# Attention scores of the first query block: two key tiles side by side in one matmul

## The chip, the cores and the metric

The kernel runs on one core of one Trainium2 chip. Its time is device microseconds (us) of one execution; the kernel before takes 1036.5 us (median of 3 runs, 1036.27 to 1037.15). Engines are named as the profile names them: PE (matmul), PEld (weight load), DVE (vector), ACT (scalar), POOL and SP (SP issues most DMAs). Each engine works through its own instructions in the order in which the program holds them.

## The reference

One decoder layer on x of 512 rows by 1024 columns, float32: a half-step gated feed-forward block, a mixer, a second half-step feed-forward block, and a final norm. The mixer has one projection whose columns are split into attention query, key and value, a small indexer, a recurrent branch and gates:

```python
def one_block(args):
    q_b, qi_b, wi_b, start = args
    ...
    _, idx = lax.top_k(score, topk)
    valid = idx <= q_pos[None, :, None]
    k_sel = jax.vmap(lambda kk, ii: kk[ii])(k, idx)
    ...
    sc = jnp.einsum("bqhd,bqkd->bqhk", q_b, k_sel).astype(jnp.float32) * (HEAD_DIM ** -0.5)
    sc = jnp.where(valid[:, :, None, :], sc, -jnp.inf)
    p = jax.nn.softmax(sc, axis=-1)
    return jnp.einsum("bqhk,bqkd->bqhd", p.astype(v.dtype), v_sel)
```

There are 8 heads of 64, all on one key and value, four blocks of 128 queries, and 128 keys are kept for each query. For the first block that is every causal key.

## The kernel before, in words

Matmul operands are held as two tiles of a rounded type: the rounded part (names ending in h or H) and what the rounding left (l or L). A product of two such numbers is three matmuls. Weights come in as `wr`, ACT rounds them to `wh`, DVE makes the remainder `wl`; so each weight tile of 128 x 1024 costs ACT and DVE one long instruction, and PE 24 matmuls of 512 columns.

The mixer is a list of jobs (ORDER in the code). Each job multiplies one weight tile by the eight input tiles and leaves a bank of results: letters i, k, e, v, x, q, g, r, a are columns of the input projection, R0 to R7 the projection of the recurrent branch, A0 to A7 that of the attention, O0 to O7 the output. All work that is not such a product (indexer, top-k, attention heads, recurrent branch) is written as generators. Between any three of a job's matmuls the program asks each generator whether its next step is due. This is decided while the program is built, by a planner: it adds up a cost for every instruction on each engine and lets a step be written down when its inputs, a psum bank, a buffer and a slot would be there, and when its engine is not booked too far ahead. So every step's place in each engine's order follows from the costs of all that stand before it. If a job needs a tile that no generator has yet written, the builder lets planned time pass without a product (`idle`) and writes down what comes due meanwhile.

A head (`head`, four at most at a time) goes through these steps for one block of queries: PE makes the score of queries against keys, two matmuls into one bank, `KH` and then `KL`, at least 256 columns wide; DVE adds the mask `am` and takes the row minimum (`pm`, custom instruction; queries are stored negated); ACT takes the exponential and its sum; DVE the reciprocal; ACT scales `pm`; PE transposes it (one per 128 keys); ACT rounds the transposed tile to `pth`, DVE makes the remainder `ptl`. When four heads are there, PE multiplies `pth` and `ptl` with the values (`VV`); ACT copies the upper half (`lo`) and DVE adds the halves into the four attention tiles. A block of queries can only begin when `top_keys` has found its kept keys on DVE: 16 rounds of MAX and MATCH_REPLACE for each block but the first. The blocks are worked one after the other. When the last head has ended, `split_attention` rounds the four attention tiles (`ath`, `atl`), and job A0 uses them.

`KH` and `KL` are made in `key_value`: each is a tile of 128 x 512 that holds the 64 key dimensions twice, so that one matmul against `QS` (rounded query in one half of the partitions, remainder in the other) sums both.

Of the kernel before, what the change touches and what calls it, by code (L numbers as in the profile page):

```python
# [10 lines left out]
F32R = mybir.dt.float32r  # L11
AF = mybir.ActivationFunctionType
# [8 lines left out]
NH = 8  # L21
HD = 64
TOPK = 128
QB = 128
# [232 lines left out]
def hybrid_kernel(ctx, tc, xt, vec, w1s, w1u, w1d, wm, wki, wrg, watt, wrnn, wout, w2u, w2d, gf, out):  # L257
    nc = tc.nc
    plan = Plan()
    V, A = plan.engine("DVE", nc.vector), plan.engine("ACT", nc.scalar)  # L260
    G, T = plan.engine("POOL", nc.gpsimd), plan.engine("PE", nc.tensor)
# [16 lines left out]
    f = lambda ap: ap.bitcast(F32)  # L278
# [5 lines left out]
    def nm(s):  # L284
        cnt[0] += 1
        return f"{s}_{cnt[0]}"

    def slot(dt=F32, name="s", last=False):
        if loans and last:
            return loans.pop()  # L290
        if mixing:
            plan.free("slot", SLOTS - 2 * COUPLES)
            held = plan.live["slot"]
            spare = [h for h in mixing if plan.key(h) not in held]
            if spare and dt is F32:
                return plan.take("slot", spare[-last])
        return plan.take("whole", plan.take("slot", big.tile([P, S], dt, tag="slot", name=nm(name))))
# [4 lines left out]
    def work(name="t", cols=S):  # L302
        return plan.take("tmp", tmp.tile([P, cols], F32, tag="tmp", name=nm(name)))

    def awork(name="a"):
        return patt.tile([P, S], F32, tag="att", name=nm(name))
# [74 lines left out]
    def waits(which, *tiles, aux=0, att=0, slots=0, key=None, mm=0, tmps=0, late=LATE, rounded=0):  # L381
        return which, tiles, aux, att, slots, key, mm, tmps, late, rounded
# [979 lines left out]
    with tc.manual_schedule(engines=ENGINES):  # L1362
# [12 lines left out]
        for k in range(KD):  # L1375
            r, h, l = (t[:, slice(k % 2 * FIRST, min(2, k % 2 + 1 + (k > 1)) * FIRST)] for t in firsts[k // 2])
# [270 lines left out]
    def aux():  # L1647
        return plan.take("aux", psaux())
# [4 lines left out]
    def att(name):  # L1653
        return plan.take("att", awork(name))
# [94 lines left out]
    def head(qb, half, j, out, before):  # L1749
        am = AM[qb]  # L1750
        nk = (qb + 1) * QB
        nw = max(nk, 2 * QB)
        qs = slice(qb * QB, (qb + 1) * QB)
        h = half * 4 + j
        KH, KL = KV
        vvv = VV[0].rearrange("p (b c) -> p b c", c=P)
        yield waits("PE", QS[h], KL, aux=1)
        sc = aux()
        T.matmul(sc[:, :nw], QS[h][:, qs], KH[:, :nw], start=True, stop=False)
        T.matmul(sc[:, :nw], QS[h][:, qs], KL[:, :nw], start=False, stop=True)  # L1760
        yield waits("DVE", sc, am, att=1)
        pm = att("pm")
        st = small.tile([P, 4], F32, tag="st", name=nm("st"))
        V.tensor_tensor_reduce(pm[:, :nk], sc[:, :nk], am[:, :nk], HD ** -0.5, 3.4e38,
                               ALU.add, ALU.min, st[:, 0:1])
        plan.drop(sc)
        if h == NH - 1:
            plan.drop(am)
        if qb == NQ - 1:
            plan.drop(QS[h])  # L1770
            if h == NH - 1:
                plan.drop(KH, KL)
        yield waits("ACT", pm)
        A.activation(pm[:, :nk], pm[:, :nk], AF.Exp, scale=-1.0, bias=st[:, 0:1], accum_out=st[:, 1:2])
        yield waits("DVE", pm)
        V.reciprocal(st[:, 2:3], st[:, 1:2])
        yield waits("ACT", st)
        A.activation(pm[:, :nk], pm[:, :nk], AF.Copy, scale=st[:, 2:3])
        yield waits("PE", pm, aux=1)
        pt = aux()  # L1780
        for b in range(qb + 1):
            T.transpose(pt[:, b * QB:(b + 1) * QB], pm[:, b * QB:(b + 1) * QB], ident)
        plan.drop(pm)
        yield waits("ACT", pt, key=before)
        if not out:
            out["n"] = 0
            for k in ("pth", "ptl"):
                out[k] = ptp.tile([P, NQ * S], F32R, tag=k, name=nm(k)).rearrange("p (b c) -> p b c", c=S)
        pth, ptl = out["pth"], out["ptl"]
        c = slice(j * QB, (j + 1) * QB)  # L1790
        p3 = pt[:, :nk].rearrange("p (b c) -> p b c", c=QB)
        A.activation(pth[:, :qb + 1, c], p3, AF.Copy)
        yield waits("DVE", pth)
        V.tensor_sub(ptl[:, :qb + 1, c], p3, f(pth[:, :qb + 1, c]))
        plan.drop(pt)
        out["n"] += 1
        if out["n"] < 4:
            return
        yield waits("PE", ptl, aux=1)
        po = aux()  # L1800
        for b in range(qb + 1):
            T.matmul(po, vvv[:, b, :], pth[:, b, :], start=b == 0, stop=False)
            T.matmul(po, vvv[:, b, :], ptl[:, b, :], start=False, stop=b == qb)
        if qb == NQ - 1 and half:
            plan.drop(VV[0])
        yield waits("ACT", po, att=1)
        ready.add((qb, half))
        lo = att("lo")
        A.activation(lo[0:64, :], po[64:128, :], AF.Copy)
        yield waits("DVE", lo)  # L1810
        v4 = lambda ap: ap[0:64, :].rearrange("p (r s c) -> p r s c", r=2, s=2)
        for r in range(2):
            for s in range(2):
                V.tensor_add(ATT[half * 2 + r][s * 64:(s + 1) * 64, qs], v4(po)[:, r, s, :], v4(lo)[:, r, s, :])
        plan.drop(po, lo)
# [5 lines left out]
    def tick():  # L1821
        for item in list(follow):
            while due(item) and advance(follow, item):
                pass
        moved = True
        while moved:
            moved = False
            heads = sum(i[2] for i in active)
            if todo and ready >= {"QS", "index"} and todo[0][0] in AM and heads < HEADS:
                qb, half, j = todo.pop(0)  # L1830
                n = qb * 2 + half - 1
                before = None if n < 0 else (n // 2, n % 2)
                active.append([None, head(qb, half, j, outs.setdefault((qb, half), {}), before), 1, SLACK])
            for item in sorted(active, key=lambda i: -i[2]):
                if due(item, item[3]):
                    moved = advance(active, item) or moved
# [111 lines left out]
    for k in ("pth", "ptl"):  # L1948
        q = ptp.tile([P, NQ * S], F32R, tag=k, name=nm("QI"))
        QI.extend(q[:, j * S:(j + 1) * S] for j in range(4))  # L1950
    KV, VV, QS = [], [], []
    gates, ATT, rnn, hrec, RN, SGR, SGA, M, MS, y2 = [], [], [], [], [], [], [], [], [], []
    YN = []

# [69 lines left out]
    def key_value(ps):  # L2024
        yield waits("DVE", ps, rstd, key="KI", tmps=1)
        kv, kw = work("kv"), joint.pop()
        V.tensor_mul(kw[64:128, :], ps[64:128, :], rstd[64:128, :])
        V.tensor_mul(kv[0:64, :], ps[0:64, :], rstd[0:64, :])
        plan.drop(ps)
        yield waits("PE", kw, aux=1, slots=3, rounded=3)  # L2030
        KH, KL = slot(F32R, "KH"), slot(F32R, "KL")
        KV.extend((KH, KL))
        VV.append(slot(F32R, "VV"))
        pv = aux()
        for b in range(NQ):
            T.transpose(pv[:, b * QB:(b + 1) * QB], kw[:, b * QB:(b + 1) * QB], ident)
        plan.drop(kw)
        for o in (slice(0, 64), slice(64, 128)):
            A.activation(KH[o, :], kv[0:64, :], AF.Copy)
        yield waits("ACT", pv)  # L2040
        vvv = VV[0].rearrange("p (b c) -> p b c", c=P)
        blocks = pv.rearrange("p (b c) -> p b c", c=QB)
        pvv = blocks[:, :, 64:128]
        A.activation(vvv[:, :, 0:64], pvv, AF.Copy)
        for o in (slice(0, 64), slice(64, 128)):
            V.tensor_sub(KL[o, :], kv[0:64, :], f(KH[0:64, :]))
        plan.drop(kv)
        V.tensor_scalar(wi.rearrange("p (b c) -> p b c", c=8), blocks[:, :, 32:40], 8 ** -0.5, 32 ** -0.5,
                        op0=ALU.mult, op1=ALU.mult)
        ready.add("wi")  # L2050
        yield waits("DVE", VV[0])
        V.tensor_sub(vvv[:, :, 64:128], pvv, f(vvv[:, :, 0:64]))
        plan.drop(pv)
# [232 lines left out]
    def split_attention():  # L2286
# [15 lines left out]
        "i": lambda t: (y, index_query(t)),  # L2302
        "k": lambda t: (y, index_key),
        "v": lambda t: (y, key_value),
        "e": lambda t: (y, merge_gate(SGR, True)),
        "q": lambda t: (yn, query(t)),
# [265 lines left out]
```

## Time and profile before

| what | value |
|---|---|
| time, median of 3 runs | 1036.5 us |
| span of the profiled execution, first to last instruction | 1034.5 us |
| PE busy in the span | 1027.6 us, 5600 matmuls |
| DVE / ACT busy in the span | 906.6 / 710.4 us |
| first and last score matmul (KH) | 454.9 and 622.7 us (start of weight load) |
| first matmul on the attention tiles (`ath`) | 639.06 us |

Of the profiled execution the span is what is known; it is 2.0 us shorter than the median of the runs. A timeline row gives start, duration, engine, line (L251 is the recording helper that all operations go through), operation, the tile written and the tiles read, sizes, and how many instructions are merged; in square brackets stands the idle time of that engine before it and what ended it. Matmuls are pipelined: their rows overlap, and what one costs PE is the distance from its start to the next start. A row of a group gives the count, the busy time in all, the mean duration in ns and the idle time before.

### The profile page before, as it was taken

What the parts mean: (1) busy time and instruction counts of PE and PEld (TensorE: products, weight loads), DVE (VectorE), ACT (ScalarE), POOL (GpSimd) and SP (SyncE); (2) the same over time, 40 slices, a digit from 0 to 9 for tenths busy, and PEclk for the clock granted to TensorE, in tenths of its full rate; (3) what the DMA queues carried; (4) which work ended last, traced back from release to release, by engine and by line L of the source; (5) the groups of instructions that cost most, each with busy time, mean ns of one, the idle gap of its engine ahead of it and who ended that gap; (6) DMA issues with size and microseconds to landing.
All of it is one profiled execution on the core that took longest, in us unless ns stands there. A gap on an engine that the chain in (4) does not pass through costs nothing.

```text
span 1034.5 us, 16004 instructions
## 1 busy us (share of the span) xinstructions
PE 1027.6 (99%) x5600; PEld 892.9 (86%) x5600; DVE 906.6 (88%) x1571; ACT 710.4 (69%) x1195; POOL 203.3 (20%) x255
## 2 busy tenths in 40 slices
PE   9999999999999999999999999999999999999997
PEld 8898888899999888888888888888988888898886
DVE  7988999889998888998989966777889999989886
ACT  8856766666766669978896674367666766657864
POOL 1613333213240011111101110013432333110000
PEclk9999999999999999999999999999999999999999
DMA  9969999897994463343469987793889999987564
GB/s 355 201 171 216 222 238 216 192 275 194 183 244 152 149 181 101 107 128 107 122 187 282 278 212 209 208 295 62 193 226 245 215 221 227 205 203 225 167 189 164
DMA packets 92257, 206.01 MB, mean 199 GB/s; under 512 B 18576, under 2 KB 25872, under 8 KB 92176
## 3 DMA queue, kind: packets, MB, share of 16 engines
q1 hardware_dynamic: 59952, 141.75, 41.0%
q0 software_dynamic: 31936, 62.93, 35.0%
q8 instruction: 44, 0.72, 0.3%
q10 hardware_dynamic: 288, 0.31, 0.1%
q14 instruction: 37, 0.30, 0.1%
HBM read 185.02 MB, written 25.17 MB: 203 GB/s over the span
## 4 chain that ended last, share of the span: by engine, by line
PE 99%; DVE 0%; DVEq 0%; issue 0%
PE mm L251 72%; PE aux L251 27%; PE aux L1340 0%; DVE xr L251 0%; DVE o L251 0%; DVE sq L251 0%; DVEq L2568 0%; DVE rs L251 0%; DVE ss L251 0%
## 5 line engine op out<-in xcount | busy, mean ns | idle before, releaser
L251 DVE TENSOR_TENSOR wl<-wr,wh 128x1024 fp32r<-128x1024 f32 (+3 forms) x154 | 183.0, 1189 | 30.6 <-ACT wh L251 30.1
L251 ACT ACTIVATE wh<-wr 128x1024 fp32r<-128x1024 f32 (+2 forms) x155 | 158.8, 1026 | 43.4 <-PE mm L251 20.0
L251 PE MATMUL mm<-cm,wh 128*128 128x512 f32 (+1 forms) x736 | 167.0, 354 | 0.0
L251 PEld LDWEIGHTS mm<-cm,wh 128*128 128x128 f32 x736 | 126.3, 190 | 15.8
L251 PE MATMUL mm<-yn,wh 128*128 128x512 f32 x420 | 130.8, 393 | 0.0
L251 PE MATMUL aux<-cm,wh 128*128 128x512 f32 (+1 forms) x472 | 119.5, 383 | 0.0
L251 PE MATMUL mm<-cm,wl 128*128 128x256 f32 x608 | 108.3, 282 | 0.0
L251 PEld LDWEIGHTS aux<-cm,wh 128*128 128x128 f32 x472 | 86.0, 188 | 15.6
L251 PEld LDWEIGHTS mm<-cm,wl 128*128 128x128 f32 x608 | 92.2, 190 | 4.7
L251 PEld LDWEIGHTS mm<-yn,wh 128*128 128x128 f32 x420 | 77.0, 188 | 14.8
L251 PE MATMUL mm<-yn,wl 128*128 128x512 f32 x210 | 81.9, 390 | 0.0
L251 PE MATMUL aux<-cm,wl 128*128 128x256 f32 x456 | 70.5, 282 | 0.0
L251 ACT ACTIVATE wh<-a 128x1024 fp32r<-128x1024 f32 (+1 forms) x68 | 57.1, 842 | 18.2 <-DVE a L251 17.2
L251 DVE TENSOR_TENSOR wl<-a,wh 128x1024 fp32r<-128x1024 f32 (+1 forms) x68 | 64.7, 952 | 5.5 <-ACT wh L251 5.0
L251 PE MATMUL mm<-yh,wh 128*128 128x512 f32 (+1 forms) x168 | 65.4, 392 | 0.0
L251 PE MATMUL mm<-yl,wh 128*128 128x512 f32 (+1 forms) x168 | 65.3, 390 | 0.0
L251 PEld LDWEIGHTS aux<-cm,wl 128*128 128x128 f32 x456 | 63.1, 191 | 1.9
L251 PE MATMUL mm<-yh,wl 128*128 128x512 f32 x160 | 62.1, 390 | 0.0
L251 ACT ACTIVATE tu<-mm 128x512 f32<-128x512 f32 (+1 forms) x57 | 28.2, 495 | 43.8 <-PE mm L251 43.7
L251 DVE TENSOR_TENSOR wl<-s,wh 128x1024 fp32r<-128x1024 f32 (+1 forms) x46 | 49.3, 1080 | 1.2 <-ACT wh L251 1.1
L251 ACT ACTIVATE wh<-s 128x1024 fp32r<-128x1024 f32 (+1 forms) x46 | 43.0, 943 | 7.1 <-PE mm L251 2.0
L251 PEld LDWEIGHTS mm<-yn,wl 128*128 128x128 f32 x210 | 39.4, 188 | 8.5
(400 smaller groups left out, 2596.8 us busy)
## 6 DMA issues: line engine op xcount, KB each, us to landing
wr<-wm SPq DMA_DIRECT2D x39, 512.0 KB, 3.6
w<-w2d SPq DMA_DIRECT2D x20, 512.0 KB, 7.0
wr<-w SPq DMA_DIRECT2D x20, 512.0 KB, 3.5
wr<-w1u SPq DMA_DIRECT2D x19, 512.0 KB, 5.9
s<-w2u SPq DMA_DIRECT2D x36, 256.0 KB, 4.4
wr<-w2u SPq DMA_DIRECT2D x18, 512.0 KB, 5.6
s<-w2u POOLq DMA_DIRECT2D x36, 256.0 KB, 6.3
s<-w1u SPq DMA_DIRECT2D x32, 256.0 KB, 4.8
```

What stands on the lines that cost most here:

```text
L251: return call(*args, **kw)
```

## The change

For the first query block only 128 keys can be seen, and yet the two score matmuls run 256 columns each. The change makes one more tile `KB`: its first 128 columns are a copy of the first 128 of `KH` (by ACT), the next 128 a copy of the first 128 of `KL` (by DVE). A head of the first block then runs one matmul of 256 columns against `KB`, which leaves the two parts of the score in two halves of the bank; a new DVE addition puts the second half and the mask into `pm`, and the custom instruction adds the first half to that. The other three blocks are as before. `key_value` asks for four free slots where it asked for three.

```diff
-        yield waits("PE", QS[h], KL, aux=1)
+        yield waits("PE", QS[h], KB[0], KL, aux=1)
         sc = aux()
-        T.matmul(sc[:, :nw], QS[h][:, qs], KH[:, :nw], start=True, stop=False)
-        T.matmul(sc[:, :nw], QS[h][:, qs], KL[:, :nw], start=False, stop=True)
+        if qb:
+            T.matmul(sc[:, :nw], QS[h][:, qs], KH[:, :nw], start=True, stop=False)
+            T.matmul(sc[:, :nw], QS[h][:, qs], KL[:, :nw], start=False, stop=True)
+        else:
+            T.matmul(sc[:, :nw], QS[h][:, qs], KB[0][:, :nw], start=True, stop=True)
+            if h == NH - 1:
+                plan.drop(KB[0])
         yield waits("DVE", sc, am, att=1)
-        pm = att("pm")
+        pm, added = att("pm"), am
+        if not qb:
+            V.tensor_add(pm[:, :nk], sc[:, nk:nw], am[:, :nk])
+            added = pm
         st = small.tile([P, 4], F32, tag="st", name=nm("st"))
-        V.tensor_tensor_reduce(pm[:, :nk], sc[:, :nk], am[:, :nk], HD ** -0.5, 3.4e38,
+        V.tensor_tensor_reduce(pm[:, :nk], sc[:, :nk], added[:, :nk], HD ** -0.5, 3.4e38,
                                ALU.add, ALU.min, st[:, 0:1])
...
-        yield waits("PE", kw, aux=1, slots=3, rounded=3)
+        yield waits("PE", kw, aux=1, slots=4, rounded=4)
         KH, KL = slot(F32R, "KH"), slot(F32R, "KL")
         KV.extend((KH, KL))
+        KB.append(slot(F32R, "KB"))
...
+        A.activation(KB[0][:, :QB], f(KH[:, :QB]), AF.Copy)
...
+        V.tensor_copy(KB[0][:, QB:2 * QB], f(KL[:, :QB]))
```

All places after the first score move with it, since the planner books the new instructions. Three places in the order matter here.

The first is PE at the first four heads of the first block, in the middle of a job on `yn`. Before:

```order
L251 MATMUL mm_5184<-yn_4144,wl_5107 128x512
L251 MATMUL aux_5199<-KH_4362,QS_4488 128x256
L251 MATMUL aux_5199<-KL_4363,QS_4488 128x256
L251 MATMUL aux_5202<-KH_4362,QS_4489 128x256
L251 MATMUL aux_5202<-KL_4363,QS_4489 128x256
L251 MATMUL aux_5205<-KH_4362,QS_4559 128x256
L251 MATMUL aux_5205<-KL_4363,QS_4559 128x256
L251 MATMUL aux_5208<-KH_4362,QS_4560 128x256
L251 MATMUL aux_5208<-KL_4363,QS_4560 128x256
L251 MATMUL mm_5184<-yn_4169,wh_5106 128x512 x2
```

Now:

```order
L251 MATMUL mm_5187<-yn_4144,wl_5110 128x512
L251 MATMUL aux_5202<-KB_4364,QS_4491 128x256
L251 MATMUL aux_5204<-KB_4364,QS_4492 128x256
L251 MATMUL aux_5206<-KB_4364,QS_4562 128x256
L251 MATMUL aux_5208<-KB_4364,QS_4563 128x256
L251 MATMUL mm_5187<-yn_4169,wh_5109 128x512 x2
```

The first heads stand at the same place, with half the matmuls. From here on the heads come later: the fifth, sixth and seventh head of the first block stood 49, 52 and 67 product matmuls behind the first four and now all stand 73 behind; the first score of the fourth block stood 559 behind and now stands 634 behind. On DVE the last of the 48 MAX rounds stood behind the 83rd `wl` of the program and now stands behind the 86th.

The second place is PE at the end of the attention. Before, the last score pair stood 57 product matmuls ahead of the first matmul on `ath`, and the last product with `VV` 21 ahead. Right ahead of `ath` stood products of job R7:

```order
L251 MATMUL mm_6960<-rh_6428,wl_6843 128x512
L251 MATMUL mm_6960<-rh_6442,wh_6842 128x512
L251 MATMUL mm_6960<-rl_6443,wh_6842 128x512
L251 MATMUL mm_6960<-rh_6442,wl_6843 128x512
L251 MATMUL mm_6960<-rh_6454,wh_6842 128x512
L251 MATMUL mm_6960<-rl_6455,wh_6842 128x512
L251 MATMUL mm_6960<-rh_6454,wl_6843 128x512
L251 MATMUL mm_7025<-ath_6989,wh_6925 128x512
```

Now the last three matmuls of R7 (`mm_6842<-rh_6376` and the two after it) are followed by attention alone. `pm_6880` is the fourth head of the last query block, `pm_6904` the fifth:

```order
L251 MATMUL mm_6842<-rh_6376,wh_6696 128x512
L251 MATMUL mm_6842<-rl_6377,wh_6696 128x512
L251 MATMUL mm_6842<-rh_6376,wl_6697 128x512
L251 MATMUL aux_6932<-ident,pm_6880 128x128 x4
L251 MATMUL aux_6945<-ident,pm_6904 128x128 x4
L251 MATMUL aux_6951<-pth_6856,VV_4365 128x512
L251 MATMUL aux_6951<-ptl_6857,VV_4365 128x512
```

Six more products of the same kind follow, and then the sixth head's transposes, the score pair of the eighth head, the transposes of the seventh and eighth, and the second half's products:

```order
L251 MATMUL aux_6951<-ptl_6857,VV_4365 128x512
L251 MATMUL aux_6960<-ident,pm_6913 128x128 x4
L251 MATMUL aux_6979<-KH_4362,QS_5184 128x512
L251 MATMUL aux_6979<-KL_4363,QS_5184 128x512
L251 MATMUL aux_6985<-ident,pm_6942 128x128 x4
L251 MATMUL aux_6995<-ident,pm_6982 128x128 x4
L251 MATMUL aux_7002<-pth_6968,VV_4365 128x512
```

Behind seven more of these stands the first matmul on `ath`. So between the last product of R7 and A0 there are now 20 transposes, 2 score matmuls and 16 products with `VV`, and no product of a job among them.

The third place is DVE in the same stretch, from the fourth head's remainder to the eighth head's reduction; `hb_104` and `hb_106` are attention tiles in their additions and the latter is the mask in the ISA rows (the custom instruction):

```order
L251 TENSOR_TENSOR ptl_6857<-aux_6932,pth_6856 128x4x128
L251 ISA pm_6942,st_6943<-aux_6922,hb_106 128x512
L251 ISA st_6943 128x1
L251 RECIPROCAL st_6943<-st_6943 128x1
L251 TENSOR_TENSOR hb_104<-aux_6951,lo_6966 64x128 x2
L251 TENSOR_TENSOR hb_106<-aux_6951,lo_6966 64x128 x2
L251 TENSOR_TENSOR ptl_6969<-aux_6945,pth_6968 128x4x128
L251 TENSOR_TENSOR ptl_6969<-aux_6960,pth_6968 128x4x128
L251 ISA pm_6982,st_6983<-aux_6979,hb_106 128x512
L251 ISA st_6983 128x1
L251 RECIPROCAL st_6983<-st_6983 128x1
L251 TENSOR_TENSOR ptl_6969<-aux_6985,pth_6968 128x4x128
```

The eighth head's reduction (`aux_6979`) now stands behind the additions of the first four heads and two remainders.

More of the change, by code (lines that the diff above doesn't have):

```diff
@@ L1950, in hybrid_kernel @@
         QI.extend(q[:, j * S:(j + 1) * S] for j in range(4))
-    KV, VV, QS = [], [], []
+    KV, KB, VV, QS = [], [], [], []
     gates, ATT, rnn, hrec, RN, SGR, SGA, M, MS, y2 = [], [], [], [], [], [], [], [], [], []
```

## The prediction

> **What bounds the kernel now.** I read the page's busy shares and chain of waits first, then windows of the mixer stage, then the timeline around the attention's end.
>
> ```profile
> PE 1027.6 (99%) x5600; PEld 892.9 (86%) x5600; DVE 906.6 (88%) x1571; ACT 710.4 (69%) x1195; POOL 203.3 (20%) x255
> PE 99%; DVE 0%; DVEq 0%; issue 0%
> ...
> 455.00:475.00 20.00, 20.00 (x98) 16.66 (x97) 19.54 (x60) 13.92 (x35) 2.64 (x5) 1.00 0.48 149
> 595.00:615.00 20.00, 20.00 (x102) 16.63 (x101) 14.45 (x40) 14.56 (x30) 2.44 (x3) 1.00 0.93 219
> 615.00:635.00 20.00, 20.00 (x100) 16.64 (x99) 10.80 (x23) 10.30 (x20) 1.66 (x2) 1.00 0.73 197
> ```
>
> The chain that ended last is PE from end to end: a matmul removed is time removed, and a pause of PE is time added, wherever it falls. In the windows (sum, then PE, PEld, DVE, ACT, POOL, clock, DMA) PE is busy for 20.00 of each 20 us: the heads are fitted in without one pause. DVE tells where the room is: 19.54 of 20 us are taken when the first block's heads run, 10.80 of 20 when the last heads do. Work that DVE cannot do at 455 to 475 us is done late.
>
> How closely the attention's end is fitted shows in the last head's own rows:
>
> ```profile
> 622.91 0.39 PE L251 MATMUL aux<-KH,QS 128*128 128x512 f32 x1
> 623.13 0.39 PE L251 MATMUL aux<-KL,QS 128*128 128x512 f32 x1
> 624.86 0.68 DVE L251 CUSTOM_DVE_ANT_0 pm<-aux,hb 128x512 f32<-128x512 f32 x1
> 625.47 0.08 DVE L251 DVE_READ_ACCUMULATOR2_ANT st<- 128x1 f32 x1
> 625.59 0.72 ACT L251 ACTIVATE pm<-pm,st 128x512 f32<-128x512 f32 x1 [1.47 <-DVE st L251]
> 626.22 0.19 ACT L251 ACTIVATION_READ_ACCUMULATOR pm<-pm,st 128x1 f32 x1
> 626.43 0.16 DVE L251 RECIPROCAL st<-st 128x1 f32<-128x1 f32 x1
> 626.78 0.71 ACT L251 ACTIVATE pm<-pm,st 128x512 f32<-128x512 f32 x1
> 629.30 0.60 PE L251 MATMUL aux<-ident,pm 128*128 128x128 f32 x4
> 629.66 0.47 PE L251 MATMUL mm<-rh,wh 128*128 128x512 f32 x1
> 629.94 0.60 ACT L251 ACTIVATE pth<-aux 128x512 fp32r<-128x512 f32 x1 [1.49 <-PE aux L251]
> 630.57 0.69 DVE L251 TENSOR_TENSOR ptl<-aux,pth 128x512 fp32r<-128x512 f32 x1 [0.86 <-ACT pth L251]
> 632.49 0.39 PE L251 MATMUL aux<-pth,VV 128*128 128x512 f32 x1
> 634.07 0.39 PE L251 MATMUL aux<-ptl,VV 128*128 128x512 f32 x1
> 634.50 0.60 ACT L251 ACTIVATE lo<-aux 64x512 f32<-64x512 f32 x1 [3.96 <-PE aux L251]
> 635.13 0.58 DVE L251 TENSOR_TENSOR ha<-aux,lo 64x128 f32<-64x128 f32 x2 [2.43 <-ACT lo L251]
> 635.74 0.58 DVE L251 TENSOR_TENSOR hb<-aux,lo 64x128 f32<-64x128 f32 x2
> 637.50 1.29 DVE L251 TENSOR_TENSOR atl<-hb,ath 128x512 fp32r<-128x512 f32 x2
> 638.83 0.39 PE L251 MATMUL mm<-rh,wl 128*128 128x512 f32 x1
> 639.06 0.39 PE L251 MATMUL mm<-ath,wh 128*128 128x512 f32 x1
> 639.29 0.39 PE L251 MATMUL mm<-atl,wh 128*128 128x512 f32 x1
> ```
>
> From its score to the first use of the attention tiles pass 16.15 us (639.06 less 622.91), filled by 57 products of R6 and R7 among others. The first `atl` is there at about 638.15 (637.50 and half of 1.29) and its user starts at 639.29: about 1 us is spare, no more.
>
> **The change part by part.** *Removed:* one of two score matmuls for 8 heads. What one costs PE is start to start:
>
> ```profile
> 511.13 0.28 PE L251 MATMUL aux<-KH,QS 128*128 128x256 f32 x1
> 511.24 0.28 PE L251 MATMUL aux<-KL,QS 128*128 128x256 f32 x1
> 511.36 0.28 PE L251 MATMUL aux<-KH,QS 128*128 128x256 f32 x1
> 511.48 0.28 PE L251 MATMUL aux<-KL,QS 128*128 128x256 f32 x1
> ```
>
> (511.48 - 511.13)/3 = 0.117 us, so 8 x 0.117 = 0.94 us come off PE. That is 0.09% of the time and could not be told from no change, for which I take 0.2% (2.1 us).
>
> *Added on DVE:* eight additions of 128 columns out of a bank and one copy of 128 x 128; on ACT one such copy. The nearest rows:
>
> ```profile
> L251 DVE TENSOR_TENSOR ptl<-aux,pth 128x128 fp32r<-128x128 f32 x8 | 2.1, 282 | 0.0
> L251 ACT ACT_TABLE_LOAD x23 | 29.5, 1283 | 1.6 <-PEq L2565 1.2
> ```
>
> Eight at 0.282 are 2.3 us of DVE; the copies are below 0.3 us each, made around 370 us, some 85 us before a score reads them, and the new wait for `KB` costs nothing. ACT's order also gains two table loads, 2 x 1.28 us. None of this is on PE's path by itself: the products of the running jobs cover it, and without that cover a head would be later by 0.28 us. The slot that `KB` holds costs nothing up to the first head, since PE's rows up to there are the same.
>
> *Moved:* the additions fall in the stretch where DVE has 0.46 us free in 20. The order shows what follows: the first block's last heads 6 to 24 products later, DVE's top-k rounds ending three weight tiles later (3 x 24 products x 0.227 = 16 us; 0.227 is about what lies between the starts at 638.83, 639.06 and 639.29), the last block starting 75 products (17 us) later. That delay passes the 1 us that was spare, and the rest is not hidden: R7's products are used up, and 20 transposes, 2 scores and 16 products with `VV` stand bare in front of A0. This is the term that decides.
>
> What PE itself issues there, up to the product with the first `atl`: a group of four transposes 0.36 (629.30 to 629.66) and 0.08 for the slower matmul behind it (0.47 against 0.39), five groups 2.2; 16 products with `VV` at (634.07 - 632.49)/7 = 0.226, 3.6; the score pair 0.45; one product on `ath` 0.23. Together 6.5 us. That work was done before too, so only the elapsed time beyond 6.5 is loss.
>
> The elapsed time from below is the chain alone, with t = 0 at the end of R7's issue. Fourth head: transposes 0.60, `pth` 0.60, `ptl` 0.69, eight products until `lo` can start 2.01 (634.50 - 632.49). The score of the eighth stands behind these on PE: sixth head's transposes 0.44, score 0.61. Then reduction 0.69, exponential with its sum 0.82 (626.41 - 625.59), reciprocal 0.16, scaling 0.71, transposes 0.60, `pth` 0.60, `ptl` 0.69, products 2.01, `lo` 0.60, additions 1.19, first `atl` 0.68. The sum is 13.7, and 15 hand-overs at 0.04 (634.46 to 634.50) make it 14.3: a loss of 14.3 - 6.5 = 7.8 us.
>
> From above, the engines' queues come in. I worked the three engines' new rows from the third block's last product on, 8.4 us ahead of t = 0, with the durations above. ACT still has two exponentials and a scaling to do before the fourth head's `pth`: 1.0 us. The eighth head's score is ready at 5.9, but DVE works on the additions of the first four heads and two remainders until 8.1: 2.1 us. In all: transposes at 0.0 and 1.8, first `VV` products at 3.0, eighth score at 5.3, its reduction at 8.1, transposes at 7.6 and 10.8, second `VV` products at 12.8, `ath` used at 16.0, `atl` at 17.4. Loss 17.4 - 6.5 = 10.9 us. The following remainders come every 0.6 us and are used every 0.68, no further loss. I take the upper value, because it is built from the order itself; both ends stay for the range.
>
> Sum on the span: 1034.5 - 0.9 + 10.9 = 1044.5 us. The median lies 2.0 above the span, which I keep: **1046.5 us, 1.0% slower**.
>
> **The rivals.** *The chain alone, without the queues:* 1036.5 - 0.9 + 7.8 = 1043.4. For it: DVE and ACT were idle for almost half of 615 to 635. Against: what they now have there is two blocks' heads at once.
>
> *PE's clock falls in the pauses.* The tail of the profile has a pause:
>
> ```profile
> 1028.14 0.28 PE L251 MATMUL aux<-wl,ch 128*128 128x256 f32 x1
> 1030.00:1032.00 2.00, 0.00 (x0) 0.00 (x0) 0.79 (x2) 0.63 (x1) 0.00 (x0) 1.00 1.00 362
> 1032.00:1033.00 1.00, 0.00 (x0) 0.00 (x0) 0.00 (x0) 0.00 (x0) 0.00 (x0) 0.78 0.91 326
> 1033.00:1034.50 1.50, 0.00 (x0) 0.00 (x0) 0.00 (x0) 0.00 (x0) 0.00 (x0) 0.50 0.00 0
> ```
>
> With 0.78 as the mean of 1.00 and 0.50 the drop to half is at 1032.56, 4.1 us after the last matmul ended. My longest pause is 2.7 us (8.1 to 10.8), so by this row the clock stays. But if transposes do not count as activity, PE is inactive from 5.9 to 12.8, and it falls. Half rate then costs the second eight products 1.8 us and the first products of A0 some more, 0.23 each; I set it at 2.5 in all, for a return to full clock within 5 us: 1049.0. [...]
>
> *More pauses elsewhere.* DVE has no room at 455 to 475, and the order is changed on all engines for 180 us. If the 2.3 us of additions and the 2.6 us of table loads reach PE in full somewhere: 1046.5 + 4.9 = 1051.4. Against: the builder inserted only steps that it took to be ready, and its like order before left no pause at all.
>
> *The end stays hidden (the other side).* Order is not time: if the chain in front of A0 took no more than PE's own 6.5 us there, only the saving is left, 1035.5, no change to tell; with the 0.08 behind a transpose group saved too it does not reach faster. It decides where the elapsed time falls below 6.5 + 0.9 = 7.4 us. For it speaks only the idle share of DVE and ACT; against it that the chain of rows is 14.3, each link of which waits for the one ahead.
>
> **How the numbers follow.** The forecast (full loss with queues) 0.45, the chain alone 0.20, the clock 0.20, more pauses 0.10, hidden 0.05. The range runs from just below the chain's 1043.4 to beyond the clock's 1049.0: 1042.5 to 1050.5 leaves out the hidden case and most of the pauses case, below 0.2. Slower by over 0.2% are the first four, 0.95; within 0.2% is most of the hidden case, 0.04; faster 0.01.
>
> **What would show it.** Eight score matmuls on `KB` and starts 0.12 apart; PE idle for 9 to 12 us in all between the last `rh` product and the first `ath` product, and nowhere else in the mixer; the waits there named as ACT `pth`, ACT `pm`, DVE `ptl` and DVE `atl`; the eighth head's reduction 2 us behind its score; clock 1.00 throughout. A granted clock below 1 near 650 us, or products 0.45 apart, would be the clock's rival. If PE is busy without a break there and the span is 1033.6, the order did not mean what I read in it.

## The result and the profile after

The changed kernel takes 1051.05 us (median of 4 runs, 1050.66 to 1051.91) against 1036.39 us for the kernel before: ratio 1.0141, 95% interval [1.0126, 1.0155]. It is 14.7 us slower, where 10.0 were forecast, and 0.55 us above the upper end of the range. One execution among the experiments' (1138.66 us, at a mean clock of 0.85) was in the slower state and is left out of the figures below.

The page of the changed kernel: span, busy shares, chain of waits.

```profile
span 1050.1 us, 16004 instructions
...
PE 1034.2 (98%) x5592; PEld 894.5 (85%) x5592; DVE 909.3 (87%) x1580; ACT 714.4 (68%) x1198; POOL 203.7 (19%) x255
...
PE 95%; DVE 2%; DMA 1%; ACT 1%; issue 0%; SPq 0%; DVEq 0%; ACTq 0%
```

Eight matmuls fewer, and yet PE is busy 6.6 us longer and the span 15.6 us longer. Nearly all of it comes from one place. The waits of PE over the whole span (what waited, for whom, us in all, times, longest):

```profile
PE aux L251 <- ACT pm L251: 5.4, 3, 2.7
PE mm L251 <- ACT ath L251: 1.2, 1, 1.2
...
PE aux L251 <- ACT pth L251: 0.7, 1, 0.7
PE mm L251 <- DVE atl L251: 0.6, 1, 0.6
...
PE aux L251 <- DVE ptl L251: 0.2, 1, 0.2
```

All of these lie at the attention's end, 8.1 us together. Of the lines left out, one (0.8 us) stands in the kernel before as well; the others, 0.9 us, are waits for weights ahead of 100 us and behind 700 us, in an execution that took 1051.91 us, 0.86 above the median. The timeline at the attention's end:

```profile
632.79 0.60 PE L251 MATMUL aux<-ident,pm 128*128 128x128 f32 x4
...
634.56 0.66 PE L251 MATMUL aux<-ident,pm 128*128 128x128 f32 x4 [1.17 <-ACT pm L251]
635.04 0.50 PE L251 MATMUL aux<-pth,VV 128*128 128x512 f32 x1
635.77 0.50 PE L251 MATMUL aux<-ptl,VV 128*128 128x512 f32 x1 [0.22 <-DVE ptl L251]
...
637.85 0.48 PE L251 MATMUL aux<-KH,QS 128*128 128x512 f32 x1
638.17 0.40 PE L251 MATMUL aux<-KL,QS 128*128 128x512 f32 x1
...
640.12 0.66 PE L251 MATMUL aux<-ident,pm 128*128 128x128 f32 x4 [1.56 <-ACT pm L251]
640.81 0.68 DVE L251 CUSTOM_DVE_ANT_0 pm<-aux,hb 128x512 f32<-128x512 f32 x1
...
643.50 1.11 PE L251 MATMUL aux<-ident,pm 128*128 128x128 f32 x4 [2.72 <-ACT pm L251]
...
645.30 0.79 PE L251 MATMUL aux<-pth,VV 128*128 128x512 f32 x1 [0.69 <-ACT pth L251]
...
646.62 0.63 PE L251 MATMUL aux<-pth,VV 128*128 128x512 f32 x1
...
648.75 0.63 PE L251 MATMUL aux<-ptl,VV 128*128 128x512 f32 x1
...
652.01 0.80 PE L251 MATMUL mm<-atl,wh 128*128 128x512 f32 x1 [0.64 <-DVE atl L251]
...
656.87 0.48 PE L251 MATMUL mm<-ath,wh 128*128 128x512 f32 x1
```

Set t = 0 at 632.79. The transposes stand at 0, 1.8, 7.3 and 10.7 us, the eighth score at 5.1, its reduction at 8.0: each within 0.3 us of the forecast. The first `VV` product starts at 2.3, earlier than the 3.0 forecast, but the second waits for `ptl` until 3.0. Then the rows grow longer: the last four transposes take 1.11 us for 0.60, and from the third on the products start 0.43 apart ((648.75 - 646.62)/5) where before they were 0.23 apart. The windows (start and end, length, then what PE, PEld, DVE, ACT and POOL were busy, the granted clock, the DMA's share and GB/s) say why:

```profile
638.60:643.50 4.90, 0.66 (x5) 0.42 (x5) 3.61 (x10) 3.37 (x7) 0.00 (x0) 0.99 0.46 86
...
643.00:644.00 1.00, 0.50 (x3) 0.51 (x4) 0.56 (x1) 0.44 (x1) 0.00 (x0) 0.69 0.00 0
644.00:656.00 12.00, 9.47 (x21) 6.08 (x20) 5.46 (x10) 4.22 (x7) 0.00 (x0) 0.50 0.01 2
656.00:658.00 2.00, 2.00 (x8) 1.61 (x7) 0.85 (x2) 0.00 (x0) 0.00 (x0) 0.74 0.81 297
```

With 0.69 and 0.74 as means of 1.00 and 0.50 in the rows from 643 and from 656 us, PE's clock is at half from 643.38 to 657.04, 13.7 us. So the loss is two things on top of each other: pauses, as forecast, and a clock that falls in them, which the forecast held for the less likely case.

### The profile page after: what moved, and what is told of

It reads as the page before. It is cut to its first block, busy times and chain, and to the rows that moved or that the text cites. A ratio compares the mean times of both kernels' runs of the same rounds, so it can differ in the third digit from the quotient of the medians.

```text
span 1050.1 us, 16004 instructions
## 1 busy us (share of the span) xinstructions
PE 1034.2 (98%) x5592; PEld 894.5 (85%) x5592; DVE 909.3 (87%) x1580; ACT 714.4 (68%) x1198; POOL 203.7 (19%) x255
## 4 chain that ended last, share of the span: by engine, by line
PE 95%; DVE 2%; DMA 1%; ACT 1%; issue 0%; SPq 0%; DVEq 0%; ACTq 0%
PE mm L251 69%; PE aux L251 26%; DMA wr<-w2d 1%; DMA wr<-w1s 1%; DVE wl L251 0%; ACT pm L251 0%; SPq L239 0%; DVE ptl L251 0%; ACT wh L251 0%; DVE xr L251 0%; DVE ha L251 0%; ACT pth L251 0%; DVE o L251 0%; DVE hb L251 0%; ACT lo L251 0%
## 5 line engine op out<-in xcount | busy, mean ns | idle before, releaser
L251 PEld LDWEIGHTS aux<-cm,wh 128*128 128x128 f32 x472 | 86.0, 188 | 15.6
```

Source lines behind the costliest of these rows:

```text
L251: return call(*args, **kw)
```

## The experiments

The theory: the loss is where the heads stand in the order (the bare end), and the clock. The rivals: the additions' own work on a DVE without room; and, for the clock, a cause other than PE's want of work. Comparisons are against the kernel before on the same chip (1036.7 us).

**The change with the order of before.** The planner is told of the old two matmuls and of nothing that is new; the chip runs the change.

```diff
-            T.matmul(sc[:, :nw], QS[h][:, qs], KB[0][:, :nw], start=True, stop=True)
+            nc.tensor.matmul(sc[:, :nw], QS[h][:, qs], KB[0][:, :nw], start=True, stop=True)
+            for k in KV:
+                plan.add("PE", 256 / 2400 + 0.0133, [sc], [QS[h], k])
...
-            V.tensor_add(pm[:, :nk], sc[:, nk:nw], am[:, :nk])
+            nc.vector.tensor_add(pm[:, :nk], sc[:, nk:nw], am[:, :nk])
```

(The two copies and the slot likewise, booked by nobody.)

> The whole change runs on the chip (tile KB, one score matmul per head of the first block, eight DVE additions), but the planner books it as if the old two matmuls stood there: the additions, the two copies and the extra slot are not booked, and the saved matmul is. The heads then stand at the same places among the products as before. Theory (the loss is the place of the heads at the attention's end, nothing else): the saving alone is left, 1036.4 - 0.9 = 1035.5 us, PE without a pause in the mixer, clock 1.00. Rival (the additions themselves cost, since DVE has no room at 455 to 475 us): 1036.4 to 1038.7, up to the 2.3 us of the additions, with pauses of PE between 455 and 535 us.

Measured: 1037.47 us, ratio 1.0007 [0.9998, 1.0016]. The 14 us are gone, so it is the order that carries them. But the saving of 0.9 us is not there either. PE waits twice between 100 and 700 us of this run (L1763 is the score on `KB`):

```profile
468.90 0.39 PE L1763 MATMUL aux<-KB,QS 128*128 128x256 f32 x1 [0.72 <-DVE st L251]
...
481.56 0.36 PE L251 MATMUL aux<-KH,QS 128*128 128x256 f32 x1 [0.55 <-DVE hb L251]
```

Here both theory and rival hold a part. The first score waits for a bank that a reduction on DVE has not yet released, in the stretch where DVE had 0.46 us free in 20; the second, shortly behind that stretch, waits for an addition of halves (`hb`) on DVE.

**The same without the additions.** One line less: the custom instruction adds the mask to the first half, and the second half of the bank is not read. The first block's scores lack the keys' remainder.

```diff
-            nc.vector.tensor_add(pm[:, :nk], sc[:, nk:nw], am[:, :nk])
-            added = pm
+            added = am
```

> The run with the order kept, with the eight additions left out (again without the keys' remainder in the first block). With them the kernel stood 0.8 us over the one before, with PE waiting 0.7 us at 468.9 and 0.5 at 481.6 for a reduction on DVE. Theory (the additions made those two waits, and the saving of 0.9 us was there under them): no wait of PE in the mixer, 1036.7 - 0.9 = 1035.8 us. Rival (the saving is not there, or the waits come from the missing booking of PE alone): 1036.7 or more, with the waits in place.

Measured: 1035.56 us, ratio 0.9990 [0.9981, 0.9999], and PE has no wait between 100 and 700 us. The saving of 0.9 us for eight matmuls is there (1.1 measured; the interval allows 0.1 to 2.0), and the additions eat it: 1037.47 - 1035.56 = 1.9 us for 2.3 us of DVE work, and the eleven runs of the one lie wholly above the eleven of the other. So even in the best order found here the change has nothing to give.

**The kernel before with only the order moved.** No instruction is added or taken away; the planner books one of the two score matmuls of a first-block head and not the other.

```diff
-        T.matmul(sc[:, :nw], QS[h][:, qs], KL[:, :nw], start=False, stop=True)
+        (T if qb else nc.tensor).matmul(sc[:, :nw], QS[h][:, qs], KL[:, :nw], start=False, stop=True)
```

> The kernel before, every instruction of it and none added, but the planner books only one of the two score matmuls of a first-block head. That alone moves the last score to the last product of R7, as in the change. Theory (the order costs, not the work): 1036.4 + 12 to 15.5 = 1048.4 to 1052 us, with 9 to 12 us of PE pauses ahead of the first product on ath and the clock at half there. Rival (what I wrote in the prediction: the additions on a full DVE are what delays the heads): without them 1036 to 1037 us.

Measured: 1053.58 us, ratio 1.0153 [1.0137, 1.0168], 1.6 us above the range I gave. The old work in a moved order is no faster than the change. Its four runs spread from 1051.20 us (mean clock 0.996) to 1054.47 (0.989): how much the clock takes differs from run to run. Two rows of its end, and its clock:

```profile
634.77 2.17 PE L251 MATMUL aux<-ident,pm 128*128 128x128 f32 x12 [1.61 <-ACT pm L251]
...
646.42 1.12 PE L251 MATMUL aux<-ident,pm 128*128 128x128 f32 x4 [3.53 <-ACT pm L251]
```

```profile
636.00:637.00 1.00, 1.00 (x6) 0.85 (x5) 0.81 (x3) 1.00 (x3) 0.00 (x0) 0.61 1.10 168
637.00:639.00 2.00, 2.00 (x5) 1.49 (x5) 0.31 (x2) 0.85 (x3) 0.00 (x0) 0.50 0.61 119
639.00:640.00 1.00, 1.00 (x4) 0.73 (x3) 0.00 (x0) 0.00 (x0) 0.00 (x0) 0.68 0.02 4
642.00:644.00 2.00, 0.70 (x2) 0.30 (x2) 1.97 (x5) 0.42 (x1) 0.00 (x0) 0.76 0.00 0
644.00:660.00 16.00, 11.05 (x25) 7.43 (x26) 6.19 (x13) 5.75 (x10) 0.00 (x0) 0.50 0.06 16
660.00:661.00 1.00, 1.00 (x5) 0.82 (x5) 0.93 (x2) 0.00 (x0) 0.00 (x0) 0.94 1.07 418
```

The clock falls twice, for 3.4 and 17.1 us, the first time (636.22) behind a single pause of 1.61 us. So the order moves, and costs this much, without any addition. The bookings can be taken one at a time in the program: the slot and the copies move no head; the additions alone move the last score from 57 products ahead of `ath` to 6; the saved matmul alone moves it to none. Either of the two would have moved the end; only the second was timed alone. The planner writes a DVE step down only if DVE is booked no more than 1.5 us beyond PE (SLACK). With PE's booked time 0.12 us shorter per head, or DVE's longer by an addition, some steps fail that test. That this is the test that fails is read from the code, not shown by a run.

**Idle products in the pauses.** The change, with 34 products that nobody reads, put between the bare steps (into A0's bank, which its first product overwrites; `now` holds that bank and the job's weights):

```diff
             while len(self.got()) <= k:
+                for _ in range(2 * (len(idles) >= 6)):
+                    nc.tensor.matmul(now[0], now[1][0][:, :P], now[1][0][:, :S], start=True, stop=True)
                 idle()
```

> The changed kernel with 34 idle products of 512 columns put into the pauses at the attention's end (into the bank of A0, which its first product overwrites): 4 ahead of the eighth score, 6 behind it, 10 and 10 behind the last two transpose groups, 4 ahead of the first product on ath. 34 x 0.227 = 7.7 us of PE work that fits into the pauses but for about 1 us. Theory (the clock fell because PE ran no products from 638.6 to 643.3): granted clock 1.00 throughout, second VV products 0.23 apart, time 1051.05 - 3.3 = 1047.7 us. Rival (the clock falls for another reason, or its fall costs nothing): 1051 to 1052 us.

Measured: 1047.18 us, ratio 1.0100 [1.0086, 1.0114]. More work and 3.9 us less time. The window of the former pause and the one behind it:

```profile
638.60:643.40 4.80, 4.80 (x25) 3.77 (x24) 3.24 (x8) 2.90 (x6) 0.00 (x0) 1.00 0.51 95
643.40:650.00 6.60, 5.80 (x26) 4.26 (x24) 2.13 (x6) 2.76 (x6) 0.00 (x0) 1.00 0.00 0
```

PE is busy for 4.80 of 4.80 us where it was 0.66 of 4.90, and the clock stays at 1.00. What is left over the kernel before, 10.5 us, is the bare end at full clock, less the saving, and with it whatever the idle products themselves hold up, which I did not separate.

**Idle transposes instead.** As above, with five transposes of a constant for two products:

```diff
+                for _ in range(5 * (len(idles) >= 6)):
+                    nc.tensor.transpose(now[0][:, :P], ident, ident)
```

> As the run with idle products, but with transposes of a constant tile in their places, 5 (0.45 us at full clock) for every 2 products: 10, 15, 25, 25, 10. Theory (transposes do not count as activity): the clock still halves near 643 us, the 25 transposes behind it take about 4.5 us instead of 2.3 and hold up the second VV products, 1053 to 1055 us. Rival (any PE instruction counts as activity, the pause itself was the cause): clock 1.00, 1047 to 1048.5 us.

Measured: 1048.39 us (three runs), ratio 1.0111 [1.0095, 1.0126]: the rival's value, and my theory falls.

```profile
638.82 1.80 PE L2295 MATMUL mm<-ident 128*128 128x128 f32 x15
...
640.89 2.89 PE L2295 MATMUL mm<-ident 128*128 128x128 f32 x25
...
638.80:646.70 7.90, 7.90 (x74) 7.88 (x73) 3.54 (x8) 3.10 (x6) 0.00 (x0) 1.00 0.16 31
```

For 7.9 us PE ran transposes and, but for the end of one score matmul, nothing else, and the clock stayed at 1.00. With the pauses filled, by products (4.80 and 6.60 us at 1.00) or by transposes (7.90 us at 1.00), it did not fall. Whether one transpose counts for as much as one product, and whether transposes alone would bring a halved clock back, no run here shows.

**The additions booked, but not run.** The order of the change, instruction for instruction, less the eight additions (the first block again without the keys' remainder):

```diff
-            V.tensor_add(pm[:, :nk], sc[:, nk:nw], am[:, :nk])
+            B.tensor_add(pm[:, :nk], sc[:, nk:nw], am[:, :nk])   # B books and does not emit
```

(The custom instruction is booked as in the change and runs on the bank's first half and the mask.)

> The changed kernel with every instruction in the place that the change gives it, but the eight DVE additions are only booked by the planner and not run (so the first block's scores lack the keys' remainder; this is the part of the computation that is left out). Theory (the additions' own 2.3 us play no part in the loss): the time of the change, 1050.5 to 1051.5 us, clock at half before A0. Rival (their DVE time is what comes out at the end): 1048 to 1049 us.

Measured: 1049.93 us, ratio 1.0128 [1.0114, 1.0142], between the two. PE's waits at the end are those of the change, but for `atl` (0.9 for 0.6):

```profile
PE aux L251 <- ACT pm L251: 5.4, 3, 2.7
...
PE mm L251 <- DVE atl L251: 0.9, 1, 0.9
```

What differs besides is the clock:

```profile
641.00:642.00 1.00, 0.00 (x0) 0.00 (x0) 0.16 (x1) 1.00 (x4) 0.00 (x0) 0.69 0.00 0
642.00:648.00 6.00, 4.58 (x12) 3.15 (x12) 1.38 (x2) 1.28 (x3) 0.00 (x0) 0.50 0.00 0
648.00:649.00 1.00, 0.49 (x2) 0.00 (x0) 0.00 (x0) 0.47 (x1) 0.00 (x0) 0.89 0.00 0
651.00:652.00 1.00, 0.88 (x3) 0.74 (x4) 1.00 (x3) 1.00 (x2) 0.00 (x0) 0.81 0.00 0
652.00:655.00 3.00, 3.00 (x8) 2.32 (x8) 2.01 (x3) 0.15 (x1) 0.00 (x0) 0.50 0.00 0
655.00:656.00 1.00, 1.00 (x5) 0.81 (x5) 0.46 (x1) 0.00 (x0) 0.00 (x0) 0.98 0.79 250
```

Worked out as above it is at half for 6.8 and 3.4 us, 10.2 in all against 13.7 in the change. The additions' own work plays no part in the pauses; whether the 1.1 us between the two kernels are wholly the clock's, I did not separate.

**Fewer bare steps.** The change with one planner constant set otherwise:

```diff
-EARLY, LATE, SLACK, HEADS = 0.3, 1.0, 1.5, 4
+EARLY, LATE, SLACK, HEADS = 0.3, 0.6, 1.5, 4
```

> The changed kernel with one planner constant set otherwise (LATE 0.6 for 1.0, how far ahead of its inputs a PE step may be written down). Behind the last product of R7 now stand only the eighth head's score pair, its transposes and the second VV products: 14 PE instructions, where the change has 38. Theory (the loss is the chain that stands bare, and the clock): chain 9.9 us less PE's own 2.9 us there, 7.0 us of pauses; 1036.7 - 0.9 + 7.0 = 1042.8 us at full clock, up to 1046 if the clock halves in the pause between score and transposes. Rival (the bare rows are not the cause): no nearer to the kernel before than 1050 us.

Measured: 1049.61 us, ratio 1.0124 [1.0110, 1.0138]. With 14 bare instructions in place of 38 it gains 1.4 us, not 5 to 8: a miss.

```profile
637.32 0.39 PE L251 MATMUL aux<-KH,QS 128*128 128x512 f32 x1
...
637.52 0.69 DVE L251 SCALAR_TENSOR_TENSOR hb<-hb,mm 128x512 f32<-128x512 f32 x1 [0.71 <-PE mm L251]
637.55 0.39 PE L251 MATMUL aux<-KL,QS 128*128 128x512 f32 x1
638.12 1.88 DVE L251 TENSOR_TENSOR ptl<-aux,pth 128x512 fp32r<-128x512 f32 x3
639.92 0.68 DVE L251 CUSTOM_DVE_ANT_0 pm<-aux,hb 128x512 f32<-128x512 f32 x1
...
642.46 1.11 PE L251 MATMUL aux<-ident,pm 128*128 128x128 f32 x4 [4.53 <-ACT pm L251]
...
650.67 0.58 PE L251 MATMUL mm<-atl,wh 128*128 128x512 f32 x1 [0.94 <-DVE atl L251]
```

I had priced the chain alone and again left out what stands ahead of the reduction on DVE: a merge and three remainders, 2.0 us (639.92 against 637.94, the end of the score, as 637.55 and 0.39). With them PE has one pause of 4.5 us, the clock falls (1.11 us for the four transposes, 0.60 at full; mean clock of the execution 0.993), and the chain takes 13.35 us (650.67 - 637.32) for the 9.9 expected; what of the remaining 1.5 us is the clock's I did not separate. What counted here is not how many instructions stand bare but how long the chain among them is (13.35 us): 24 instructions fewer took only 1.4 us off.

## Why the prediction was wrong, point by point

**Right:** the saving (0.9 us; 1.1 measured with the additions out of the way); that the last heads stand bare ahead of A0; the pauses. By the forecast `atl` is used 17.4 us after R7's last product, 10.9 us lost. The change needed 19.2 (652.01 - 632.79), and but for the first `VV` product every step up to 10.7 us was within 0.3 us of its forecast, before the clock fell. The run with the clock held lost 10.5 net of the saving, against 10.0 forecast. The waits add up to 8.1 us where 9 to 12 were named; part of the loss shows as longer busy rows instead.

**Wrong, and the step that sank it:** "My longest pause is 2.7 us (8.1 to 10.8), so by this row the clock stays." The pause was 2.72 us, and the clock fell in it, at 643.38. The one row I had, the tail's 4.1 us, tells how long after the last matmul the clock fell once; it does not bound how short a pause can do it. The length of a single pause was the wrong measure: PE was busy for 0.66 of the 4.9 us around the fall, with one group of four transposes between pauses of 1.56 and 2.72 us, and that was not enough. With only the order moved the clock fell behind a pause of 1.61. The rival that I did price (2.5 us, chance 0.20) was the case that came, but not under the condition that I set for it, and its size was too small as well. From t = 10.7 on, the full clock would have had `atl` at about 17.3 by my estimate (10.7 and the forecast's 17.4 - 10.8), so 1.9 us were lost up to there; A0's next eleven products took 4.86 us (656.87 - 652.01) for 2.5, another 2.4. Together 4.3: -0.9 + 10.8 (17.3 - 6.5) + 4.3 = 14.2 of the 14.7 measured. The 2.5 us stood on a return to full clock within 5 us, which I had assumed and which no run shows: the clock was at half for 13.7.

**Wrong, without harm to the number:** "the additions fall in the stretch where DVE has 0.46 us free in 20. The order shows what follows". The order moves as far without any addition, by the saved matmul's booking alone, which I had not named; booked alone the additions would move it nearly as far. The forecast of the time stood on the order itself, not on why it moved. The condition that the rival set for the fall, that transposes do not count as activity, was an assumption that no run shows, and one speaks against it: with nothing but transposes and the end of one score matmul on PE the clock stayed at 1.00 for 7.9 us. The queue on DVE at 455 to 475 us does matter, but for another thing: in the old order it costs the change its saving (PE waits 0.72 us for DVE at 468.90).

**The other rivals.** The chain alone (1043.4): the queues were there; the eighth head's reduction stood 2.2 us behind the end of its score (640.81 against 638.57), for 2.1 to 2.2 in the forecast. More pauses elsewhere: none in the mixer. Hidden end: no.

## What to carry to other kernels

Where a planner writes the order, a change is the order that it makes: compare the places of late, dependent steps first, and look for the point where the work that covered them runs out. One small difference in the planned costs can move a stage's end; test the same work in the moved order, and the new work in the old order, before any mechanism is believed. The bare chain on PE cost its pauses here and then the clock (at half for 13.7 us): price both. The longest pause alone did not tell when the clock falls: it fell behind a single pause of 1.61 us in one kernel, and in a pause of 2.72 in another, with PE busy for 0.66 of the 4.9 us around the fall; take PE's share of idle time over a few us with it.

## What the runs showed of the hardware

The stretches at half clock took 3.4 and 17.1 us in the kernel with only the order moved, 6.8 and 3.4 with the additions not run, 13.7 in the change; that is 1, 5, 2, 1 and 4 times 3.42 (17.1/5). Between two stretches the clock was at full for about as long as the shortest of them, in the first kernel from 639.64 to 643.04 and in the second from 648.22 to 651.62, 3.40 us each. These are lengths worked out from mean clocks of five stretches in three executions; why they agree, no run here shows.

The rows below give PE's busy time in windows of about this length ahead of a fall or a return of the clock. Three are of the change, and behind the last dots stands the one ahead of the first fall with only the order moved:

```profile
636.55:639.96 3.41, 2.02 (x11) 1.33 (x9) 1.65 (x6) 2.80 (x6) 0.63 (x1) 1.00 0.66 114
639.96:643.37 3.41, 0.66 (x4) 0.42 (x4) 2.21 (x6) 1.94 (x5) 0.00 (x0) 1.00 0.23 44
...
653.61:657.03 3.42, 3.42 (x10) 2.65 (x9) 1.29 (x2) 0.00 (x0) 0.00 (x0) 0.50 0.28 84
...
632.81:636.22 3.41, 1.80 (x12) 1.07 (x11) 1.87 (x8) 3.41 (x8) 0.81 (x1) 1.00 1.02 179
```

The clock stayed at full behind the window with 2.02 us of PE work, fell behind those with 0.66 and 1.80, and came back behind one that was busy throughout. These windows are too few for a share at which it turns, all the more as most of the 1.80 us are transposes. Nor does a run here show why the four runs with the order moved spread from 1051.20 to 1054.47 us.

I had not expected that the clock would come back so late while PE worked: in the change it stayed at half through 644 to 656 us with PE busy for 9.47 of 12.00. And with transposes and the end of one score matmul alone it stayed at 1.00 for 7.9 us.
